# Splitting the second sums of a 2x2 average pool so that scaling overlaps with adding

## The chip, the cores and the metric

One core of one Trainium2 chip runs the kernel. The metric is device time in microseconds; before the change it was 3103.25 us, the median of 3 runs (3103.14 to 3103.47). Profiles are of one execution each, whose span is some 1.8 us shorter than the time of that run.

## The reference

An average pool, window 2x2, stride 2, on float32 of shape (32, 128, 256, 256), to (32, 128, 128, 128):

```python
window = x[:, :, h_start:h_start + 2, w_start:w_start + 2].copy()
output[:, :, i, j] = np.mean(window, axis=(2, 3))
```

The kernel must read 1073.74 MB and write 268.44 MB; the arithmetic is three adds and one scaling for each output element.

## The kernel before

A tile is 128 partitions x 32 groups; a group is one pair of image rows (512 values in, 128 out). There are 127 whole tiles and a rest as large as one, done in three parts. Two input buffers and two result buffers take turns (a third result buffer is for the rest). The sync engine (SP) issues the loads, the vector engine (DVE) adds, the scalar engine (ACT) scales and issues the stores. Synchronization is by hand: `take(engine, sem, n)` waits until `sem` is at least n and takes n off.

```python
def load(t, b):
    sp.dma_start(out=ins[b], in_=xt[t]).then_inc(loaded[b], 16)

def sums(it, dst):
    dve.tensor_add(out=it[:, :, 0:w], in0=it[:, :, 0:w], in1=it[:, :, w:]).then_inc(halfway)
    take(dve, halfway)
    dve.tensor_add(out=dst, in0=it[:, :, 0:w:2], in1=it[:, :, 1:w:2]).then_inc(summed)

def tile_sums(b):
    take(dve, stored[b], 16)     # the store of two tiles ago has left res[b]
    take(dve, loaded[b], 16)
    sums(ins[b], res[b])

def scale_store(t, b, landed):
    take(act, summed)
    act.sem_inc(free[b])         # SP may load into ins[b] again
    scale(res[b])                # act.mul by 0.25, in place
    take(act, scaled)
    act.dma_start(out=ot[t], in_=res[b]).then_inc(landed, 16)
# ... (the loops over the tiles, and the rest, are cut)
```

## Time and profile before

| | before |
|---|---|
| median time | 3103.25 us |
| DVE busy | 1679.3 us, 54% |
| ACT busy | 464.5 us, 15% |
| two DMA queues, share of 16 engines | 80.2% + 19.9% |
| a tile starts every | 24.20 us |
| median landing, store / load | 30.8 / 31.5 us |

The lines behind this table are in the prediction below. A "landing" is the time from the issue of a transfer to the arrival of its semaphore; it holds whatever the transfer waits before it moves (the same loads take 31.5 us here and 47.0 in `moves_only` below). In a timeline line the first two numbers are start and duration, and the square bracket has how long the engine idled before it.

### The profile page before, as it was taken

To read this page: it belongs to the slowest core of one execution; us is meant where nothing else is said; L and a number is where in the kernel's file an instruction comes from. 1 tells how busy PE (TensorE), PEld (TensorE's weight loads), DVE (VectorE), ACT (ScalarE), POOL (GpSimd) and SP (SyncE) were. 2 spreads that over 40 slices of the span, in tenths; PEclk is the share of its full clock that TensorE was granted. 3 is DMA by queue.
4 is the path that set the end of the run, shared out by engine and by line. 5 is a ranking of instruction groups with operands and counts; after the bars stand their busy time and mean duration, and the time that the engine had idled before them with its cause. 6 is when DMAs were issued, how large, how long until landed. Compare 5 with 4: busy or idle time off the path is not lost. (4 is left out here: it accounts for less than half of the span.)

```text
span 3101.7 us, 2612 instructions
## 1 busy us (share of the span) xinstructions
DVE 1679.3 (54%) x260; ACT 464.5 (15%) x131; POOL 0.2 (0%) x4
## 2 busy tenths in 40 slices
DVE  4555555555555555555555555555555555555556
ACT  1111111111111111111111111111111111111111
POOL 0000000000000000000000000000000000000000
DMA  9999999999999999999999999999999999999999
GB/s 415 437 439 426 436 439 423 439 438 424 439 434 428 439 431 431 439 426 436 439 426 436 437 428 437 439 426 440 436 425 438 438 427 436 438 424 439 434 428 416
DMA packets 37440, 1342.19 MB, mean 433 GB/s; under 512 B 4160, under 2 KB 4160, under 8 KB 4416
## 3 DMA queue, kind: packets, MB, share of 16 engines
q1 hardware_dynamic: 19008, 1077.94, 80.2%
q10 hardware_dynamic: 18432, 264.25, 19.9%
HBM read 1073.74 MB, written 268.44 MB: 433 GB/s over the span
## 5 line engine op out<-in xcount | busy, mean ns | idle before, releaser
L88 DVE TENSOR_TENSOR in_tile<-in_tile 128x8192 f32<-128x8192 f32 (+1 forms) x130 | 1112.9, 8560 | 1396.8 <-DVEq L68 1396.8
L98 ACT ACTIVATE res<-res 128x4096 f32<-128x4096 f32 (+1 forms) x130 | 463.3, 3564 | 2595.3 <-ACTq L68 2595.3
L90 DVE TENSOR_TENSOR res<-in_tile 128x4096 f32<-128x4096 f32 (+1 forms) x130 | 566.7, 4359 | 19.1
L98 ACT ACT_TABLE_LOAD x1 | 1.3, 1283 | 36.5 <-ACTq L68 36.5
L240 POOL MEMSET const-uint8-127<- 128x1 uint8 x1 | 0.1, 102 | 0.0
L240 POOL MEMSET const-bfloat16-1.0<- 128x1 bf16 x1 | 0.1, 101 | 0.0
L240 POOL MEMSET const-float32-0.0<- 128x1 f32 x1 | 0.1, 98 | 0.2 <-issue 0.2
L240 POOL MEMSET const-float32-1.0<- 128x1 f32 x1 | 0.1, 98 | 0.0
## 6 DMA issues: line engine op xcount, KB each, us to landing
out_dram<-res ACTq DMA_DIRECT2D x125, 2048.0 KB, 30.8
in_tile<-in_x_dram SPq DMA_DIRECT2D x1, 4096.0 KB, 17.8
in_tile<-in_x_dram SPq DMA_DIRECT2D x2, 2048.0 KB, 24.4
out_dram<-res SPq DMA_DIRECT2D x2, 2048.0 KB, 20.2
in_tile<-in_x_dram SPq DMA_DIRECT2D x127, 31.5
out_dram<-res ACTq DMA_DIRECT2D x1, 1024.0 KB, 7.8
out_dram<-res ACTq DMA_DIRECT2D x2, 512.0 KB, 5.3
```

The lines of the kernel that those rows point to most:

```text
L88: dve.tensor_add(out=it[:, :, 0:w], in0=it[:, :, 0:w], in1=it[:, :, w:]).then_inc(halfway)
L90: dve.tensor_add(out=dst, in0=it[:, :, 0:w:2], in1=it[:, :, 1:w:2]).then_inc(summed)
L98: act.mul(out=dst, in_=dst, mul=0.25).then_inc(done)
L240: nc = _bacc.Bacc("TRN2", target_bir_lowering=False, num_devices=1)
```

## The change

The intent: ACT needn't wait until the whole second sum is done. DVE makes it in two halves of 16 groups, and ACT scales the first half while DVE adds the second. The input buffer is still freed after the second half, and the store still takes the whole tile.

```diff
-        dve.tensor_add(out=dst, in0=it[:, :, 0:w:2], in1=it[:, :, 1:w:2]).then_inc(summed)
+        for g in halves(pieces):
+            dve.tensor_add(out=dst[:, g], in0=it[:, g, 0:w:2], in1=it[:, g, 1:w:2]).then_inc(summed)
...
+    def tile_scale(b, done, frees=True):
+        for k, g in enumerate(halves()):
+            take(act, summed)
+            if k and frees:
+                act.sem_inc(free[b])
+            scale(res[b][:, g], done)
+
     def scale_store(t, b, landed):
-        take(act, summed)
-        act.sem_inc(free[b])
-        scale(res[b])
-        take(act, scaled)
+        tile_scale(b, scaled)
+        take(act, scaled, 2)
         act.dma_start(out=ot[t], in_=res[b]).then_inc(landed, 16)
```

(`pieces` is 2 for whole tiles and 1 for the rest; the last two whole tiles, which SP stores, wait for two halves in the same way.)

More of the change, by code (lines that the diff above doesn't have):

```diff
@@ L82, in _pool_2x2, with halves, sums @@
         a = b
+    def halves(pieces=2):
+        if pieces == 1:
+            return [slice(None)]
+        return [slice(0, TILE // 2), slice(TILE // 2, TILE)]
     def load(t, b):
         sp.dma_start(out=ins[b], in_=xt[t]).then_inc(loaded[b], 16)
-    def sums(it, dst):
+    def sums(it, dst, pieces=1):
         dve.tensor_add(out=it[:, :, 0:w], in0=it[:, :, 0:w], in1=it[:, :, w:]).then_inc(halfway)
         take(dve, halfway)
-        dve.tensor_add(out=dst, in0=it[:, :, 0:w:2], in1=it[:, :, 1:w:2]).then_inc(summed)
+        for g in halves(pieces):
+            dve.tensor_add(out=dst[:, g], in0=it[:, g, 0:w:2], in1=it[:, g, 1:w:2]).then_inc(summed)
     def tile_sums(b):
@@ L94, in tile_sums @@
         take(dve, loaded[b], 16)
-        sums(ins[b], res[b])
+        sums(ins[b], res[b], 2)
     def scale(dst, done=scaled):
         act.mul(out=dst, in_=dst, mul=0.25).then_inc(done)
+    def tile_scale(b, done, frees=True):
[4 more added lines that the diff above has]
+            scale(res[b][:, g], done)
     def scale_store(t, b, landed):
-        take(act, summed)
-        act.sem_inc(free[b])
-        scale(res[b])
-        take(act, scaled)
+        tile_scale(b, scaled)
+        take(act, scaled, 2)
         act.dma_start(out=ot[t], in_=res[b]).then_inc(landed, 16)
@@ L126, in _pool_2x2 @@
         for k, t in enumerate((whole - 2, whole - 1)):
-            take(sp, held[k])
+            take(sp, held[k], 2)
             sp.dma_start(out=ot[t], in_=res[t % 2]).then_inc(tail, 16)
@@ L150, in _pool_2x2 @@
         for k, t in enumerate((whole - 2, whole - 1)):
-            take(act, summed)
-            if k == 0:
-                act.sem_inc(free[t % 2])
-            scale(res[t % 2], held[k])
+            tile_scale(t % 2, held[k], frees=k == 0)
         for a, b, _ in parts:
```

## The prediction

> **What bounds the kernel now.** I read the page first for a busy engine, then the DMA queues, then one stretch of the timeline to see which wait starts a tile, and last the end of the run.
>
> ```profile
> span 3101.7 us, 2612 instructions
> DVE 1679.3 (54%) x260; ACT 464.5 (15%) x131; POOL 0.2 (0%) x4
> DMA  9999999999999999999999999999999999999999
> ...
> q1 hardware_dynamic: 19008, 1077.94, 80.2%
> q10 hardware_dynamic: 18432, 264.25, 19.9%
> ```
>
> No compute engine is near its limit: the vector engine (DVE) is busy 54%, the scalar engine (ACT) 15%. The two DMA queues, q1 with the loads and q10 with most of the stores, fill 80.2 + 19.9 = 100.1% of the time of the 16 DMA engines. That looks like the bound. The view by stretches, from the first store to the last whole tile, agrees: DMA share 1.00 at 434 GB/s over 3020 of the 3102 us (columns: stretch, length, busy time of DVE, ACT, POOL, clock, DMA share, GB/s).
>
> ```profile
> 41.50:3062.00 3020.50, 1639.57 (x250) 451.93 (x125) 0.00 (x0) 1.00 1.00 434
> 3062.00:3098.00 36.00, 26.60 (x8) 7.71 (x5) 0.00 (x0) 1.00 0.96 411
> ```
>
> The timeline of two tiles shows which transfer lets a tile begin (start, duration, engine, line):
>
> ```profile
> 997.86 4.42 DVE L90 TENSOR_TENSOR res<-in_tile 128x4096 f32<-128x4096 f32 x1
> 1002.48 3.62 ACT L98 ACTIVATE res<-res 128x4096 f32<-128x4096 f32 x1 [20.58 <-ACTq L68]
> 1002.64 97.13 SPq L85 DMA_DIRECT2D in_tile<-in_x_dram  x5
> 1006.34 0.34 ACTq L105 DMA_DIRECT2D out_dram<-res  x1
> 1013.22 8.69 DVE L88 TENSOR_TENSOR in_tile<-in_tile 128x8192 f32<-128x8192 f32 x1 [10.94 <-DVEq L68]
> ...
> 1037.42 8.69 DVE L88 TENSOR_TENSOR in_tile<-in_tile 128x8192 f32<-128x8192 f32 x1 [10.94 <-DVEq L68]
> ```
>
> and the DMA issues give the median time to landing:
>
> ```profile
> out_dram<-res ACTq DMA_DIRECT2D x125, 2048.0 KB, 30.8
> in_tile<-in_x_dram SPq DMA_DIRECT2D x127, 31.5
> ```
>
> A tile starts every 1037.42 − 1013.22 = 24.20 us. The load issued at 1002.64 lands near 1002.64 + 31.5 = 1034.1, but the DVE starts that buffer only at 1037.42. The store issued at 1006.34 lands near 1006.34 + 30.8 = 1037.1. So the wait that ends last is the one for the store of two tiles before, which frees the result buffer; the load came about 3.0 us sooner. This is the trap of the case: a store issued earlier seems to shorten the loop. But stores are issued 24.20 us apart and take 30.8, so for 6.6 us of each period two are queued; loads take 31.5, so for 7.3 us two loads are queued. Neither queue runs dry[...].
>
> [...]
>
> ```profile
> L90 DVE TENSOR_TENSOR res<-in_tile 128x4096 f32<-128x4096 f32 x127 | 561.9, 4425 | 18.6
> L98 ACT ACTIVATE res<-res 128x4096 f32<-128x4096 f32 x127 | 459.2, 3616 | 2587.9 <-ACTq L68 2587.9
> L90 DVE TENSOR_TENSOR res<-in_tile 128x2048 f32<-128x2048 f32 x1 | 2.3, 2293 | 0.1
> L98 ACT ACTIVATE res<-res 128x2048 f32<-128x2048 f32 x1 | 1.9, 1909 | 3.2 <-ACTq L68 3.2
> ```
>
> **The change part by part.** These last rows hold the sizes before (128x4096) and the new ones (128x2048).
>
> *Vector engine.* 127 second sums become 254. Busy time: 127 × (2 × 2.293 − 4.425) = +20.4 us, so 1679.3 becomes about 1700. On the clock less: at the end of the run an add that waits for nothing starts 0.08 us before the one ahead of it has ended (3085.72 + 2.29 = 3088.01 against a start at 3087.93), so a pair takes 2.21 + 2.29 = 4.50 in place of 4.42, +0.08 us a tile. DVE idles 10.9 us before every tile, which hides it.
>
> *Scalar engine.* 127 × (2 × 1.909 − 3.616) = +25.7 us, 464.5 becomes about 490, hidden in 20.6 us of idle time a tile. The first half runs beside the second DVE half: it starts 0.20 after its sum and needs 1.91, a sum of 2.11 against 2.21, so it is out of the way in time.
>
> *The store.* Now it is issued 1006.34 − 1002.28 = 4.06 us after the second sum has ended (997.86 + 4.42 = 1002.28). Afterwards: 0.08 + 0.20 + 1.91 + 0.24 (1006.34 less the end of the scaling, 1006.10) = 2.43 us. Each store is issued 1.63 us sooner after its tile starts.
>
> *The load.* The buffer is freed after the second half, when ACT's sequencer sees it, so the load's issue moves by +0.08 us. It has some 7 us of queued load in front, so nothing comes of it.
>
> *The DMA engines.* Bytes, packets and queues are the same. A tile is 8.389 + 2.097 = 10.486 MB, 128 tiles at 24.19 us are 3096.3 us, and the remaining 5 us are the start of the first load and the last landing. Nothing in the change is in this sum: −1.63 us on a store's issue turns into +1.63 us in its queue. The first store goes out some 1.8 us earlier (41.54 before); over that time a fifth of the DMA goes to it, which delays the load under way by about 0.4 us, and those bytes are no longer to be moved later. So the gap between a load's landing and the store's, 3.0 us, should shrink to about 0.8 us.
>
> *The end.* The last stretch runs at a DMA share of 0.96. The last whole tile may start 1 to 2 us sooner for DVE, since the store it waits for lands sooner, and its small parts follow. But they queue behind the same bytes. I put −0.3 us on this and +0.1 on everything else. Sum: 3103.25 − 0.2 = 3103.0 us.
>
> **The rivals.** (1) *The loop of result buffers binds.* The chain is DVE start, sums, scaling, store issue, landing, DVE start: 48.4 us for two tiles, of which 1.63 would go. That is 0.8 us a tile, some 100 us in all, near 3000 us. For it: the store does land last, 0.3 us before each DVE start. Against it: that would need 434 × 3103 / 3000 = 449 GB/s, above all that was seen over a long stretch, from engines already busy 100%. (2) *The extra instructions bind:* 0.08 us for 127 tiles, +10 us, or 3113, if DVE were in the loop with nothing to spare. Against it: DVE is idle 1396.8 us, and the store's 1.63 us is a larger gain in the same loop. (3) *The DMA rate shifts a little,*[...]: ±0.1% is ±3 us. Nothing in the profile says which sign. (4) *The tail is worth its whole shift:* −1.5 us, if the last store's issue rather than the queue ahead sets the end.
>
> **Range and chances.** I predict 3103.0 us, with 3100.5 to 3105.5 eight times in ten: (3) and (4) set the width, the three runs of before differ by only 0.33 us. Faster by over 2% would need rival (1) in most of its strength, 1%. Slower by over 2% needs a new stall of half a microsecond on every tile that reaches the DMA, 1%. Within 2%: 98%.
>
> **What would show each step.** DVE count 260 + 127 = 387 and busy near 1700; ACT count 258 and near 490; the store's issue 2.4 us after the second half-sum ends. Both queues still at about 100% together, 434 GB/s, tiles 24.2 us apart. The stores' median landing rises from 30.8 to about 32.4 (30.8 + 1.63) and the loads' from 31.5 to about 33.8 (31.5 + 2.2 by the smaller gap + 0.08), because what waits longer in a queue is what the change gained. If instead the stores' landing stays at 30.8 and tiles come under 24 us apart, the loop bound it and I am wrong; if the DMA share falls under 0.99 in the middle, a new stall has opened.

Three passages are cut from this text where marked, since they rest on what no trace or run of this case shows: a paragraph of figures and rules on the DMA engines, DVE and ACT, with the step that a tile's load and its store finish at one pace; a clause on what the landing time mostly is; and a clause on what might shift the DMA rate. The rows after the first cut are the profile's own durations, 2.293 and 1.909 us for the halves, and the fifth of the DMA that goes to the first store is the 19.9% of the second queue. 3103.25 − 0.3 + 0.1 came, rounded, to 3103.0 us, and the two small terms were estimates.

## The result and the profile after

The changed kernel took 3102.76 us (median of 6 runs, 3102.09 to 3103.99), the kernel before 3103.27 us beside it (6 runs, 3102.26 to 3103.47). The ratio is 0.9999, with a 95% interval of 0.9987 to 1.0012: no difference. A ratio here is the mean time of one kernel's runs over that of the other's of the same rounds, so it isn't quite the ratio of the medians.

From the page of the kernel after, its busy times and queues (share of the DMA engines' time last):

```profile
DVE 1688.1 (54%) x387; ACT 490.3 (16%) x258; POOL 0.2 (0%) x4
...
q1 hardware_dynamic: 19008, 1077.94, 80.3%
q10 hardware_dynamic: 18432, 264.25, 19.9%
```

DVE has 127 more instructions and ACT 127 more, and the DMA engines are as full as before, within 0.1%. The timeline of two tiles of the kernel after:

```profile
999.57 1.91 ACT L106 ACTIVATE res<-res 128x2048 f32<-128x2048 f32 x1 [0.36 <-ACTq L68]
999.74 48.70 SPq L92 DMA_DIRECT2D in_tile<-in_x_dram  x3
1001.72 0.34 ACTq L118 DMA_DIRECT2D out_dram<-res  x1
1010.25 8.69 DVE L95 TENSOR_TENSOR in_tile<-in_tile 128x8192 f32<-128x8192 f32 x1 [10.87 <-DVEq L68]
1019.09 4.50 DVE L98 TENSOR_TENSOR res<-in_tile 128x2048 f32<-128x2048 f32 x2
1021.50 1.91 ACT L106 ACTIVATE res<-res 128x2048 f32<-128x2048 f32 x1 [20.02 <-ACTq L68]
1023.77 1.91 ACT L106 ACTIVATE res<-res 128x2048 f32<-128x2048 f32 x1 [0.36 <-ACTq L68]
1025.92 0.34 ACTq L118 DMA_DIRECT2D out_dram<-res  x1
1034.42 8.69 DVE L95 TENSOR_TENSOR in_tile<-in_tile 128x8192 f32<-128x8192 f32 x1 [10.84 <-DVEq L68]
```

The overlap works. The first scaling (1021.50 to 1023.41) runs while DVE is adding (1019.09 to 1023.59), and the store goes out 1025.92 − 1010.25 = 15.67 us after the tile starts. Before, the store of the tile that started at 1013.22 went out at 1030.54, 17.32 us after it:

```profile
1030.54 0.34 ACTq L105 DMA_DIRECT2D out_dram<-res  x1
```

So each store is issued 1.65 us sooner. But the next tile starts at 1034.42, still 24.17 us after the one before. Where the 1.65 us went is in the DMA issues of the kernel after (the last number is the median us to landing):

```profile
out_dram<-res ACTq DMA_DIRECT2D x125, 2048.0 KB, 32.5
in_tile<-in_x_dram SPq DMA_DIRECT2D x127, 34.3
```

A store takes 32.5 us to land in place of 30.8: it leaves earlier and waits longer. By itself this proves nothing: in both profiles a tile starts some 0.25 us after the store that it waits for has landed, so as long as tiles keep their beat, what a store gains at its issue must reappear in its landing. Why the beat stays is for the experiments to show. In the view by stretches nothing has moved but the busy times of DVE and ACT (columns: stretch, length, DVE, ACT, POOL, clock, DMA share, GB/s):

```profile
41.50:3062.00 3020.50, 1648.26 (x375) 477.43 (x250) 0.00 (x0) 1.00 1.00 434
```

At the end of the run, the last small store is issued at 3094.17 us where before it was 3096.44, some 2.3 us sooner. The profiled span is shorter by 1.4 us (3100.3 against 3101.7). But the runs of the two kernels scatter by 1.2 us (before) and 1.9 us (after), their ranges overlap, and the profile after is of the fastest of its six runs (3102.09 us), while the profile before is of a run of 3103.51 us. So no gain is claimed from that.

### The profile page after: what moved, and what is told of

It is laid out like the page before. It is cut to its first block, busy times and chain, and to the rows that moved or that the text cites. A ratio compares the mean times of both kernels' runs of the same rounds, so it can differ in the third digit from the quotient of the medians.

```text
span 3100.3 us, 2993 instructions
## 1 busy us (share of the span) xinstructions
DVE 1688.1 (54%) x387; ACT 490.3 (16%) x258; POOL 0.2 (0%) x4
## 3 DMA queue, kind: packets, MB, share of 16 engines
q10 hardware_dynamic: 18432, 264.25, 19.9%
## 5 line engine op out<-in xcount | busy, mean ns | idle before, releaser
L106 ACT ACTIVATE res<-res 128x2048 f32<-128x2048 f32 (+1 forms) x257 | 489.0, 1903 | 2569.5 <-ACTq L68 2569.5
L98 DVE TENSOR_TENSOR res<-in_tile 128x2048 f32<-128x2048 f32 (+1 forms) x257 | 575.4, 2280 | 19.0
L106 ACT ACT_TABLE_LOAD x1 | 1.3, 1283 | 34.3 <-ACTq L68 34.3
## 6 DMA issues: line engine op xcount, KB each, us to landing
out_dram<-res ACTq DMA_DIRECT2D x125, 2048.0 KB, 32.5
in_tile<-in_x_dram SPq DMA_DIRECT2D x1, 4096.0 KB, 19.9
in_tile<-in_x_dram SPq DMA_DIRECT2D x127, 34.3
```

What stands on the lines that cost most here:

```text
L98: dve.tensor_add(out=dst[:, g], in0=it[:, g, 0:w:2], in1=it[:, g, 1:w:2]).then_inc(summed)
L106: act.mul(out=dst, in_=dst, mul=0.25).then_inc(done)
```

## The experiments

Two theories stood against each other. **Q**: the DMA engines are full, and time won by a store is spent in its queue. **L**: the loop of result buffers (DVE start, sums, scaling, store, landing, DVE start) binds, and what leaves that loop leaves the time. Under L the change should have been worth some 100 us. Twelve kernels ran, in three groups, each on a chip of its own; each group shares its runs of the kernel before, which took 3103.3 to 3103.4 us.

### late_wait: take the wait that ends last out of the way

```diff
 def tile_sums(b):
-    take(dve, stored[b], 16)
     take(dve, loaded[b], 16)
     # sums: first add; take(dve, halfway)
+    take(dve, stored[b], 16)
     # second add
```

(Shortened: in the kernel the semaphore is handed to `sums`; the comments stand for its lines.)

> The kernel before, with the DVE's wait for the store of two tiles ago moved from ahead of the first add to just ahead of the second, the only one that writes the result buffer. Theory Q (the DMA engines are full, time won by a store is spent in its queue): 3103 us within 0.1%; the DVE starts a tile on its load instead, some 3 us earlier relative to it, and the stores' median time to landing rises from 30.8 us by about those 3 us. Theory L (the loop of result buffers binds): the loop of two tiles loses 8.84 us, the first add, and the time falls by well over 100 us.

Measured: 3103.56 us (3102.47 to 3103.76, 5 runs), ratio 1.0 (0.9987 to 1.0014). The stores and loads of this kernel:

```profile
out_dram<-res ACTq DMA_DIRECT2D x125, 2048.0 KB, 33.8
in_tile<-in_x_dram SPq DMA_DIRECT2D x127, 34.5
```

The landing rose by the 3.0 us that Q named, and the time stayed. Here no tile waits for its store any more when it starts, so this rise isn't forced by the arithmetic. The wait that ended last could be removed from the start of each tile without gain: it ended last, but it did not bind.

### moves_only: keep the transfers, drop the arithmetic

```diff
-        sums(ins[b], res[b])
+        sums(ins[b][:, 0:1], res[b][:, 0:1])
...
-        scale(res[b])
+        scale(res[b][:, 0:1])
```

(The same for the scaling of the last two whole tiles; the two result buffers are zeroed once at the start; the result is wrong.)

> The kernel before with full loads and stores, but the sums and the scaling work on 1 of 32 groups (wrong result on purpose): nearly all compute is gone, the transfers and their waits stay. Q: 3097 to 3103 us, because the transfers alone set the time. L: the loop loses some 15 of its 48 us, and the time would fall by hundreds of us.

Measured: 3102.91 us (3102.80 to 3103.76, 5 runs), ratio 0.9999 (0.9985 to 1.0012). Its busy times:

```profile
DVE 111.6 (4%) x262; ACT 44.6 (1%) x131; POOL 0.2 (0%) x4
```

With 1568 us of DVE work and 420 us of ACT work gone, the time is the same. This is the strongest single proof of the bound: a change that leaves these transfers as they are and touches only the arithmetic has nothing to win. The freed time shows up as waiting of the loads: their median landing here is 47.0 us in place of 31.5, while that of the stores is 30.9.

### Delays in front of the store

If margin is what the change gives, a delay should show it. An extra scaling by 1.0 (the result stays right) goes in front of each store that ACT issues, in the kernel before and in the changed one:

```diff
         take(act, scaled)
+        act.mul(out=res[b], in_=res[b], mul=1.0).then_inc(scaled)
+        take(act, scaled)
         act.dma_start(out=ot[t], in_=res[b]).then_inc(landed, 16)
```

For `delay3` the two lines run three times; for `delayhalf` they work on 16 of the 32 groups; `delay1_late_wait` has them in the kernel of `late_wait`. The last four of the expectations below were written when the results of the first three were known.

`delay1_before`:

> The kernel before, with one more scaling by 1.0 of the whole result tile on ACT ahead of each store: each store is issued about 3.85 us later. Q: same within 0.2%[...]; landing time falls to about 27 us. L: half of 3.85 us a tile, +245 us, 3350 us.

`delay3_before`:

> As delay1_before with three more scalings: each store 11.6 us later. Q: [...]the store queue runs dry and the loop binds now[...], so 3350 to 3530 us, with the DMA share under 0.95. L: half of 11.6 us a tile, about 3840 us.

`delay3_after`:

> The same three extra scalings put into the changed kernel. Q: where the loop binds the change must be worth what it takes out of it: 1.63 us of two tiles, 0.8 us a tile, about 100 us below delay3_before (3%). If the change were worth nothing for another reason (an issue held up, a wait that moved), it would equal delay3_before.

`delayhalf_before`:

> The kernel before with one extra scaling of half a result tile ahead of each store: 2.15 us later (1.91 and 0.24). How near was the kernel before to the edge? If it had some 3 us of margin: 3103 us. If it stood at the edge: by the slope of the whole delay (153 us for 3.85 us) up to 85 us more, 3190 us.

`delayhalf_after`:

> The changed kernel with the same delay of 2.15 us: net 0.5 us against the kernel before without a delay. Expected 3103 us within 0.3%, whichever of the two held for the kernel before.

`delay1_after`:

> The changed kernel with the one extra scaling of the whole result tile that cost the kernel before 153 us (4.9%). If what that delay cost came by way of the wait for the result buffer, the 1.63 us that the change takes out must come back as margin: a net delay of 3.85 - 1.63 = 2.2 us against before, so clearly under 3256 us, between 3103 and 3190. If the delay costs by something else (ACT's own time, the release of the input buffer), about 3256 us again.

`delay1_late_wait`:

> The whole delay of 3.85 us, but with the wait for the result buffer moved behind the first add, which gives that loop 8.8 us. If the delay cost the kernel before its 153 us through this wait: 3103 us within 0.3%. If by another way (ACT, the store queue running dry by itself): about 3256 us.

| extra delay of the store, as expected | in the kernel before | in the changed kernel |
|---|---|---|
| 0 | 3103.3 us | 3102.76 us, ratio 0.9999 |
| 2.15 us (delayhalf) | 3104.37 us, ratio 1.0005 (0.9990 to 1.0019) | 3103.37 us, ratio 1.0000 (0.9986 to 1.0014) |
| 3.85 us (delay1) | 3256.22 us, ratio 1.0488 (1.0472 to 1.0504) | 3118.34 us, ratio 1.0040 (1.0014 to 1.0066) |
| 11.6 us (delay3) | 3724.35 us, ratio 1.2002 (1.1984 to 1.2020) | 3586.37 us, ratio 1.1563 (1.1545 to 1.1580) |
| 3.85 us with the late wait | 3103.71 us, ratio 1.0000 (0.9986 to 1.0014) | |

Each ratio is to the kernel before without a delay, in the same group; the two kernels with 3.85 us ran in different groups, so their ratios are compared. The delays that the timelines show, from the start of a tile to the issue of its store, are a little smaller: 2.0, 3.7 and 11.2 us (19.33, 21.04 and 28.54 us in the kernel before, against 17.32). The text below uses these. The four runs of delay1_after scatter from 3102.87 to 3123.84 us, as would be expected at an edge.

Lines from the timeline of delay1_before and one from its view by stretches show the loop binding:

```profile
1005.97 8.69 DVE L88 TENSOR_TENSOR in_tile<-in_tile 128x8192 f32<-128x8192 f32 x1 [3.67 <-DVEq L68]
...
1027.01 0.34 ACTq L108 DMA_DIRECT2D out_dram<-res  x1
1040.16 8.69 DVE L88 TENSOR_TENSOR in_tile<-in_tile 128x8192 f32<-128x8192 f32 x1 [20.92 <-DVEq L68]
...
1057.09 8.69 DVE L88 TENSOR_TENSOR in_tile<-in_tile 128x8192 f32<-128x8192 f32 x1 [3.67 <-DVEq L68]
```

```profile
41.50:3062.00 3020.50, 1561.00 (x238) 860.76 (x239) 0.00 (x0) 1.00 0.99 412
```

The even beat is gone: in this stretch one tile starts 34.19 us after the last, and the next 16.93 us after that. A tile's store is issued 1027.01 − 1005.97 = 21.04 us after its start, and the next tile of that buffer starts 1057.09 − 1027.01 = 30.08 us later: a loop of 51.12 us for two tiles, where it was 48.4. The DMA share is 0.99 all the same; only the rate, 412 GB/s in place of 434, shows the loss. Whether the slower engines add to the loss or only follow from the uneven beat, no run settles.

What follows:

1. The loop of result buffers is real, but in the kernel before it had margin. With 2.0 us more in it nothing happens; with 3.7 us more it costs 153 us. `delay1_late_wait` shows that the cost came by way of that wait: the same delay, with the wait moved behind the first add, costs nothing.
2. The expectation for delay1_before, "same", was wrong, and so were L's 3350 us and Q's landing of about 27 us (29.7 measured). The margin that I had counted on came from an estimate of mine that no trace showed, and it was too large: 3.7 us of delay were more than there was. The timeline of before had a better number: the very first store, issued at 41.54 us with nothing ahead of it, is followed by the start of its buffer's next tile at 69.88, which is 28.3 us later at most. Where the margin really ends is read from the table: before the change between 2.0 and 3.7 us, after it near 3.8 (the delay in delay1_after), where one run lost nothing and three lost 11 to 20 us. The two differ by the 1.65 us of the change if the first is near 2.1. The profiles of delayhalf_before and delay1_after show median landings of 28.8 and 28.7 us, but this is no separate proof: while the beat holds, a landing is what the beat leaves over, as said above. In delay1_before, where the beat broke, it was 29.7.
3. So the change did take 1.65 us out of the loop, as it should. Where the loop binds, it is worth something: at 3.7 us of delay 4.9% of loss becomes 0.4%, and at 11.2 us the changed kernel is 138 us (3.7%) faster than the kernel before with the same delay. Of this I had expected about 100 us. The 138 us are 2.2 us for each pair of tiles, of which the earlier issue makes 1.64 (28.54 to 26.90 us after the tile's start in the two timelines). What shortens the rest of the loop by some 0.5 us isn't settled.
4. delay3_before was expected at 3350 to 3530 us and took 3724. The tiles came in pairs there, 58.4 us a pair: 28.54 us from a tile's start to its store's issue (1015.12 to 1043.66) and 29.88 us from there to the next tile of that buffer (1073.54). The expectation had 29.1 for the first (17.5 + 11.6); for the second it had the estimate that is cut above, which was too small, so the landing is what was mis-sized. That the DMA share would fall under 0.95 was right: 0.87, at 361 GB/s.

### Half loads: the same change with less to move

```diff
-        sp.dma_start(out=ins[b], in_=xt[t]).then_inc(loaded[b], 16)
+        sp.dma_start(out=ins[b][:, 0:TILE // 2], in_=xt[t][:, 0:TILE // 2]).then_inc(loaded[b], 16)
```

(For all but three whole tiles; the rest of each buffer is left over from earlier tiles, so the result is wrong. half_sums_only has DVE's halves, but ACT waits for both and scales the tile in one. From the expectation of half_before the terms of a sum are cut where marked, as one of them, the landing, was an estimate that no trace showed; the sum came to the 2180 us that are left.)

`half_before`:

> The kernel before, but all loads except three bring only the first half of a tile (the result is wrong on purpose; sums, scaling and stores unchanged). A tile then moves 6.29 MB in place of 10.49, 14.5 us at 434 GB/s, so the DMA need not bind. Expected by Q: the loop of result buffers, [...]some 2180 us, DMA share about 0.85. If the load loop or the DVE (13.3 us a tile) binds instead, 1850 to 2000 us.

`half_after`:

> The same half loads in the changed kernel. Q: if the loop of result buffers binds there, the change is worth 0.8 us a tile, about 100 us (4 to 5%) below half_before. If the change is worthless in itself, equal; if the DVE or the free-load loop binds, 5 to 10 us slower by the 0.08 us of the extra add.

`half_sums_only`:

> Half loads and one part of the change alone: the second sums come in two halves, but ACT waits for both and scales the whole tile. Only the cost is left: 0.08 us in the loop for each tile, +5 to +10 us over half_before (0.2 to 0.5%). If splitting costs more than the trace shows (an extra wait or semaphore), more than that.

Measured: half_before 2132.69 us (2127.35 to 2143.03), half_after 2128.91 us (2127.49 to 2132.83), half_sums_only 2139.71 us (2129.80 to 2145.27), 4 runs each, ratios to the kernel before 0.6876 (0.6857 to 0.6895), 0.6864 (0.6853 to 0.6874) and 0.6884 (0.6869 to 0.6898). The intervals overlap (those of half_after and half_sums_only only just), so no difference between the three is claimed, and the cost of the extra add (5 to 10 us expected) can't be told from the scatter. The experiment missed its aim. Stretches of half_before and of half_after:

```profile
60.00:2050.00 1990.00, 1594.52 (x244) 437.70 (x121) 0.00 (x0) 1.00 0.96 384
```

```profile
60.00:2050.00 1990.00, 1608.96 (x367) 465.99 (x244) 0.00 (x0) 1.00 0.96 386
```

The DMA engines are still 96% busy, not 85% as expected, though they move only 384 to 386 GB/s. The change's 1.65 us came back in part here too: the stores' median landing is 16.4 us in half_after against 15.2 in half_before. Whether the DMA engines, at a lower rate, or the loop bind here is not settled. The tests that tell the theories apart are moves_only, late_wait and the delays.

## Why the prediction was right

- **The bound.** That the DMA engines, not the loop, set the time was right, and moves_only shows it: 3102.91 us with hardly any arithmetic. That the forecast of 3103.0 us came within 0.3 us of the median is partly luck, as the runs scatter by 1.2 and 1.9 us.
- **The wait that ends last is the store's, but it does not bind.** late_wait shows both halves: moved away, it left the time where it was, and the landing grew by 3.0 us. Rival (1), 3000 us, was false for this kernel and true for one whose margin is used up (the delays).
- **The store's issue.** −1.63 us predicted, −1.65 measured (17.32 to 15.67). The stores' landing: 32.4 predicted, 32.5 measured.
- **The load's landing.** 33.8 predicted, 34.3 measured. The step with the wrong size is the gap between load and store: I had it shrink from 3.0 to 0.8 us, by a first store 1.8 us earlier and a load 0.4 us later. The first store was issued 2.1 us earlier (39.42 in place of 41.54) and landed after 27.4 us in place of 28.1, and the load beside it took 29.9 us as before. In the timeline after, the load issued at 999.74 lands near 999.74 + 34.3 = 1034.04 and the store near 1001.72 + 32.5 = 1034.22, a gap of 0.2.
- **DVE's busy time.** +20.4 us predicted, +8.8 measured. The sum took two whole durations for each pair; the profile counts the time in which two adds overlap once (the 255 adds of the half size and their mean of 2.288 us make 583.4 us, and it counts 573.0). The clock time of the pair was the right term: 127 × (4.495 − 4.425) = 8.9 us, with 4.49 and 4.50 us in the timeline. It had no effect on the time, being hidden, so rival (2), 3113 us, was false. ACT: 490.3 us, as predicted; its halves lie 0.36 us apart and don't overlap.
- **The queue's margin.** The prediction took landing time in excess of 24.2 us as time in a queue (6.6 us a period). That both queues overlap was right (a load takes 31.5 us to land and a store 30.8, and each is issued every 24.2), but not all of the 6.6 us can be spent: 2.0 us cost nothing and 3.7 us cost 153, as the delays show.
- **The end.** The prediction gave it −0.3 us and said that the last stores queue behind the same bytes. DVE began the last whole tile 2.3 us sooner (3065.64 in place of 3067.97), a little more than the 1 to 2 us named, and the last issue came 2.3 us sooner, but the time moved by less than the runs scatter. Rival (4), the whole shift, isn't seen in the medians (0.5 us apart); the size of the effect stays open.

## What to carry to other kernels

Before shortening the chain behind the wait that ends last, ask whether the resource behind that wait is already full: if it is, an earlier issue only lengthens the landing (here 1.65 us earlier and 1.7 us longer). Those two numbers describe it but don't prove it; a kernel with the same transfers and hardly any arithmetic does. A wait that binds nothing today still has a margin, and delays of known size measure it: here between 2.0 and 3.7 us before and near 3.8 us after. Such a change is insurance, not speed, and moving the wait behind the first add, without an extra instruction, buys at least as much of it: 3.7 us of delay cost nothing at all there.

## What else these runs measured

- One more instruction cost little: a pair of halves takes 4.495 us on DVE against 4.425 for the whole (70 ns more), and two scalings of half a tile back to back at the start of the run take 3.71 us against 3.62 (90 ns). The profile's busy sum then grew by the small number where the halves touch (DVE: +8.8 us, 70 ns for each of 127) and by about twice it where they lie apart (ACT: +25.8 us, 203 ns for each).
- The busy share of the DMA engines and their rate did not move together. With half loads the share is 0.96 at 384 GB/s, so by an estimate from these two a fully busy set of engines would move 384 / 0.96 = 400 GB/s; in delay1_before it is 0.99 at 412 GB/s, 416 when full; in the kernel before 1.00 at 434. A share near 1 is not by itself a proof that the rate is the best one. What slows the engines there no run of this case settles.
- With nothing ahead of it in its queue and loads beside it, the first 2 MB store landed after 28.1 us in the kernel before and 27.4 in the changed one, while the beat of load and store together is 24.2 us.
